# Where the weights of 72 TensorE products lie in SBUF, relative to the moving operands

## The chip, the cores and the metric

The kernel runs on one core of a Trainium2 chip. The metric is the device time of one execution in microseconds, the median of several runs. Profiles come from one execution recorded by the hardware profiler; its times are counted from the start of its span.

## What is computed

One decoder layer on 1024 prompt rows and 64 sample rows (1088 tokens in all, model width 1024). Cut to what matters here:

```python
a, q, k, v, g_a, g_b = split(rms_norm(x, ln1) @ w_in)
A = pooled(a) @ w_pa                       # causal multi-scale pooling
B = attended(q, k, v) @ w_pb               # dilated sliding-window attention, three groups
h = x + (sigmoid(g_a) * A + sigmoid(g_b) * B) @ w_o
y = h + square(relu(rms_norm(h, ln2) @ w_up)) @ w_down
```

The parts of interest are the gates `g_a`, `g_b` (1024 by 2048 weights) and the up projection `w_up` (1024 by 4096). All is float32 outside; the products are made of pairs of reduced-precision parts.

## The kernel before

**Precision.** Each float32 operand is split into a high part in a rounded format and a low part with the rest (`split`, L116 on ScalarE and L117 on VectorE). A product then takes three passes: high by high, high by low, low by high (`PASSES`).

**Seven products for eight.** The gate and the up projection are computed by a block scheme of the Strassen-Winograd kind. Tokens are cut into two halves (544 each) and the 1024 input channels into two halves (four tiles of 128 channels each); a panel of 256 output columns is cut into two tiles of 128. Each panel takes products of a weight block (128 columns by four channel tiles) with a token block. The products are named by their moving operand:

- `11` and `21`: blocks of the normed input, first token half. They lie in the two tiles `act` (high and low), whose channel tiles are 1088 words apart.
- `22`: a block of the second token half; `T1`: a sum of token blocks written in place of another one. Both lie in `act` too, 544 words further on.
- `T2`, `T3` and `T4`: further sums of token blocks. They lie outside `act`, four channel tiles of 544 words each, one after the other: T2 and T3 in `places`, T4 in a tile of its own (`gt4` in the gate stage, `t4`, shown as `t`, in the up stage).

One product (`products`, through `by_halves`, L1292) is 24 matmuls: two runs of twelve, the first for 264 tokens, the second for the other 280; in each run three passes over four channel tiles. Every matmul is preceded by its own load of weights (128 by 128), which the profile shows as PEld.

**Stages.** Attention and the first products of the gates share the time to 445 us. From there eight gate panels run with the products T1, T2, T3, 22 and T4 each. Then come the two branch projections (`pab`), the output projection (`ph`, L200) and the up projection: first the products 11 and 21 of panels 0 to 7, then T1, T2, T3, 22 and T4 of those eight, then panels 8 to 15 with all seven products in the order 11, T1, 21, T2, T3, 22, T4. The down projection (`pd`, L2069) ends the kernel.

**Where the weights lie.** `put_weights` writes a block's high and low parts into a spot of 1152 words; there are five spots, two in tiles of their own (`gapart` for the gates, `apart` for the up projection) and three in `places`. Inside a spot the four channel tiles of the high part start at `at + step * k`, those of the low part 128 words after them. The table `W_AT` gives `at` and `step` by product. The source of a block is a quarter of a weight panel or a sum of two quarters that VectorE has made.

**What sets the order.** TensorE's order is written out by hand: a queue of products, whose weights are prepared three products ahead (`run(ahead=3)`) and whose raw panels are asked for about seven products ahead. PSUM tiles are drained behind each product by ScalarE or VectorE.

Addresses below are counted in float32 words along a partition. The tiles `act`, `places`, `gapart`, `apart`, `gt4` and `t4` of the moving operands and weights all start at multiples of 64 words, as do the spots.

Of the kernel before, what the change touches and what calls it, by code (L numbers as in the profile page):

```python
# [15 lines left out]
P = 128  # L16
# [21 lines left out]
def decoder_step(ctx, tc, i, o):  # L38
# [76 lines left out]
    def split(dst_hi, dst_lo, src):  # L115
        ins = s_.activation(dst_hi, src, AF.Copy)  # L116
        v_.tensor_tensor(dst_lo, src, dst_hi.bitcast(F32), op=ALU.subtract)  # L117
        return ins
# [14 lines left out]
    def gate_quarter(f, a):  # L133
        return gate_panel(f).rearrange("p (k n) -> p k n", k=KD)[:, 4 * a:4 * a + 4, :P]
# [8 lines left out]
    def line_up(src, name, *after, width=None):  # L143


        wt = places[:, place[0] % 3]
        place[0] += 1
        width = width or src.shape[1]
        for a, key in zip(range(0, width, 512), after):
            coming_up.append(dict(width=width, src=src, name=name, a=a, key=key, wt=wt, raw=None))  # L150
        ask_ahead()
        return wt
# [33 lines left out]
    def behind_pe(ins, mm=None):  # L186

        tc.add_manual_dep(ins.ins, (mm or last_mm[0]).ins.name,
                          mybir.DependencyInfo(mybir.DependencyClass.Sync, mybir.DependencyReason.DATA), reason="pace")
# [349 lines left out]
    ap = pb.enter_context(tc.tile_pool(name="att", bufs=1, reuse_waits="tile"))  # L539
# [596 lines left out]
    for g in (2, 1, 0):  # L1136
# [42 lines left out]
        for blks in ((8, 0), (1,), (2,), (3,), (4,), (5,)) + (((6, 7),) if g else ((6,), (7,))):  # L1179
# [7 lines left out]
            elif not g and 3 in blks:  # L1187
                wg_first = line_up(lambda a: gate_quarter(a // 512 % 2, a // 1024), "ga0",
                                   *((0, 7, j) for j in (0, 0, 1, 1)), width=2048)
# [98 lines left out]
    def by_halves(out, terms, lhs, rhs, first=True, between=None):  # L1288

        for c in range(2):  # L1290
            for n, term in enumerate(terms):
                last_mm[0] = t_.matmul(out[c], lhs(*term), rhs(*term, c), start=(first and n == 0),  # L1292
                                       stop=(n == len(terms) - 1), skip_group_check=not first)
            if between:
                between()

    TERMS = [(a, b, k) for a, b in PASSES for k in range(4)]

    def products(x, A, Bv, first, between=None):
        by_halves(x, TERMS, lambda a, b, k: A[a][:, k], lambda a, b, k, c: Bv(b, k, c), first, between)  # L1300

    def put(t, src, marks):
        marks.append(split(t[:, 0], t[:, 1], src))
        return t

    W_AT = {"11": (8, 256), "21": (8, 256), "T1": (40, 256), "22": (40, 256), "T2": (8, 288), "T3": (8, 288), "T4": (8, 288)}

    def weights_at(at):
        return spots[:, at:at + 1152]

    def put_weights(t, src, marks, key):
        at, step = W_AT[key]
        if len(src.shape) == 2:
            src = by_tile(src)
        hi, lo = (bass.AP(tensor=t.tensor, offset=t.offset + at + P * s, ap=[t.ap[0], [step, 4], [1, P]]) for s in range(2))
        marks.append(split(hi, lo, src))
        return hi, lo

    queue, lazy, loads = [], [], {}
# [33 lines left out]
    def row_tile(n, name):  # L1353
        return rr(rows_p, [P, H], F32, name=f"g{n}_{name}", tag=f"g{n}", bufs=2)
# [65 lines left out]
    def put_gate(src, key):  # L1420
        spot[0] += 1
        return put_weights((apart + [weights_at(1152 * n) for n in (2, 1, 0)])[(spot[0] - 1) % 5], src, marks_g, key)
# [7 lines left out]
    by_tile = lambda t: t.rearrange("p (k n) -> p k n", n=P)  # L1430

    def gate_group(f):
# [34 lines left out]
        def post4():  # L1467
# [3 lines left out]
        loads.setdefault(max(0, len(queue) - 4), []).append(get_back)  # L1471
        enqueue(lambda: summed(1, quarter(f, 1, 0), quarter(f, 1, 1), ALU.add),
                lambda A: products(fresh(5), A, B["T1"], True), post5, (lambda: load_gate(f)) if f else None, 7)
        enqueue(lambda: summed(2, by_tile(sums[1]), quarter(f, 0, 0), ALU.subtract),
                lambda A: products(fresh(6), A, B["T2"], True), post6)
        enqueue(lambda: summed(3, quarter(f, 0, 0), quarter(f, 1, 0), ALU.subtract),
                lambda A: products(fresh(7), A, B["T3"], True), post7)
        enqueue(lambda: summed(4, quarter(f, 0, 1), by_tile(sums[2]), ALU.subtract),
                lambda A: products(outs(q["x5"]), A, B["22"], False), post3)
# [10 lines left out]

    def put_first(n):
        if n < 4:
            return [by_tile(wg_first[:, s, 512 * n:512 * n + 512]) for s in range(2)]
        if n < 16:
            w = put_weights(weights_at(1152 * ((n + 1) % 3)), raw_first.pop(n), marks_g, "11")
            behind_pe(marks_g[-1])
            return w
# [4 lines left out]
    for n in range(3):  # L1502
        ready[n] = put_first(n)
    for n, (f, a) in enumerate(order):
        fetch_first(n + 5)
        if a == 0:
            open_x[f] = bank_pair(f"pg{f}")
        products(open_x[f], ready.pop(n), B["21" if a else "11"], a == 0, between=step)
        ready[n + 3] = put_first(n + 3)
        t = row_tile(1 + a, f)  # L1510
        for c in range(2):
            s_.copy(t[:, part(c)], open_x[f][c])
        dma_st(g_d[f, 0][:, half(0)] if a else pg_d[f], t)
        if n in (3, 5, 7, 9):
            split_sums((n - 3) // 2)
        if n in (0, 1, 4, 6):
            fetch_sums((0, 1, 4, 6).index(n))
        if n % 4 == 3 and psx is None and not active and not waiting:
            finish_attention()
        if psx is not None and n > 8:  # L1520
            prepare_main()
        if n == 13:
            for f in range(8):
                gate_group(f)
            for n_prep in range(3):
                got[n_prep] = queue[n_prep][0]()
        if n == 14:
            for load in loads.pop(0):
                load()
# [106 lines left out]
    at = len(queue)  # L1636
# [116 lines left out]
    def put_up(src, key):  # L1753
        spot[0] += 1
        t = put_weights(up_spots[spot[0] % 5], src, marks_f, key)
        in_time(marks_f[-1])
        return t
# [340 lines left out]
    for g, n_rows in ((2, 30), (1, 21), (0, 30)):  # L2098
        src, dst = i[f"cache_kv{g + 1}"], o[f"kv{g + 1}_sample"]
# [111 lines left out]
```

## Time and profile before

| What | us |
|---|---|
| Median of three runs | 1410.89 |
| Lowest and highest run | 1408.71, 1411.37 |
| The profiled execution | 1410.39 |
| Its span | 1408.6 |
| First product of the gates | 384.8 |
| Gate panels with T1, T2, T3, 22, T4 | 444.92 to 565.30 |
| Branch projections | 565.30 to 637.0 |
| Output projection | 637.0 to 734.8 |
| Up projection, products 11 and 21 of panels 0 to 7 | 734.8 to 784.44 |
| The other five products of these panels | 784.44 to 904.82 |
| Panels 8 to 15, all seven products | 904.82 to 1072.52 |
| Down projection | 1072.52 to about 1404 |

How the views are read: PE is TensorE's matmuls and PEld its loads of weights. A matmul's row gives its duration of some 280 to 290 ns, but matmuls follow each other every 120 to 130 ns and overlap, so what counts is the time from the start of one to the start of the next, or from the start of one product to that of the next. In the timeline, rows of equal instructions are merged under the form of the first, so a row of 24 holds 12 matmuls of 264 columns and 12 of 280. Names stand without their numbers: `pg` and `pz` are PSUM tiles of the gates and of the up projection, and the names behind the arrow are the tiles that hold the moving operand and the weights.

### The profile page before, as it was taken

Reading aid. Unit: us, or ns where it says so; the run is one execution under the profiler, and the core shown is the slowest. Engines: PE = TensorE matmul, PEld = TensorE weight load, DVE = VectorE, ACT = ScalarE, POOL = GpSimd, SP = SyncE. Lnnn points to the kernel's source line nnn. Section 1 sums busy time; section 2 is a strip of 40 time slices with the busy share of each in tenths; the row PEclk is TensorE's granted clock in tenths of the full one; section 3 lists DMA queues with packets and bytes.
Section 4 is the critical chain, followed back from the end, with each engine's and each line's share of the span. In section 5 each row is a group of like instructions: output and inputs, shape, how many; then the busy total and the mean of one; then the engine's idle time right before and its main releaser. Section 6 shows DMA issues by size and latency. Waiting matters only on the chain.

```text
span 1408.6 us, 29517 instructions
## 1 busy us (share of the span) xinstructions
PE 1397.0 (99%) x11101; PEld 1348.7 (96%) x11101; DVE 970.1 (69%) x1766; ACT 758.8 (54%) x1962; POOL 233.9 (17%) x330
## 2 busy tenths in 40 slices
PE   9999999999999999999999999999999999999998
PEld 9988887888999999999999999999999999999998
DVE  7788675676776767876468678665665686664565
ACT  8557755777865233564336455554554544443443
POOL 0722265466500100000001000000000000000100
PEclk9999999999999999999999999999999999999999
DMA  6322778745377777975458668856658987777674
GB/s 214 117 96 103 219 212 220 195 140 145 105 253 228 252 227 238 315 240 171 140 199 278 230 224 267 266 191 220 237 196 286 326 276 260 228 247 228 200 265 168
DMA packets 184541, 303.58 MB, mean 216 GB/s; under 512 B 26567, under 2 KB 90509, under 8 KB 182350
## 3 DMA queue, kind: packets, MB, share of 16 engines
q1 hardware_dynamic: 181326, 258.04, 57.3%
q0 software_dynamic: 3072, 43.65, 9.4%
q8 instruction: 87, 1.43, 0.4%
q14 instruction: 56, 0.46, 0.1%
HBM read 231.55 MB, written 113.73 MB: 245 GB/s over the span
## 4 chain that ended last, share of the span: by engine, by line
PE 92%; DMA 3%; DVE 2%; ACT 1%; POOL 1%; SPq 1%; issue 1%; DVEq 0%; POOLq 0%; ACTq 0%
PE pz L1292 24%; PE pd L2069 24%; PE pg L1292 12%; PE ph L200 7%; PE pab L1292 5%; PE pqk L200 5%; PE pv L200 3%; PE a L328 3%; PE pq L200 1%; PE pk L200 1%; DMA raw_qkv<-in_w_in_dram 1%; DMA pcv<-in_cache_kv_dram 1%; PE pog0b L717 1%; PE sg0b L684 1%; PE tpg0b L703 0%
## 5 line engine op out<-in xcount | busy, mean ns | idle before, releaser
L2069 PE MATMUL pd<-places 128*128 128x272 f32 x2688 | 331.7, 287 | 0.0
L2069 PEld LDWEIGHTS pd<-places 128*128 128x128 f32 x2688 | 331.6, 188 | 0.0
L116 ACT ACTIVATE places<-raw_d 128x544 fp32r<-128x544 f32 (+1 forms) x176 | 111.3, 647 | 159.5 <-DMA raw_d<-z_d 58.6
L117 DVE TENSOR_TENSOR places<-raw_d,places 128x544 fp32r<-128x544 f32 (+1 forms) x176 | 123.1, 713 | 93.3 <-ACT places L116 91.3
L2109 POOL DMA_DIRECT2D out_kv_sample_dram<-in_cache_kv_dram x96 | 47.1, 490 | 794.6 <-ACT places L116 582.2
L1292 PE MATMUL pz<-act,places 128*128 128x280 f32 (+1 forms) x1080 | 139.4, 287 | 0.0
L1292 PEld LDWEIGHTS pz<-act,places 128*128 128x128 f32 x1080 | 135.9, 188 | 0.0
L200 PE MATMUL ph<-act,places 128*128 128x280 f32 (+1 forms) x768 | 96.6, 287 | 0.0
L200 PEld LDWEIGHTS ph<-act,places 128*128 128x128 f32 x768 | 96.0, 188 | 0.1
L1292 PE MATMUL pg<-act,places 128*128 128x264 f32 (+1 forms) x576 | 75.6, 288 | 0.0
L1292 PEld LDWEIGHTS pg<-act,places 128*128 128x128 f32 x576 | 72.6, 188 | 0.6 <-issue 0.3
L1292 PE MATMUL pz<-places,apart 128*128 128x264 f32 (+1 forms) x528 | 68.7, 289 | 0.0
L1292 PEld LDWEIGHTS pz<-places,apart 128*128 128x128 f32 x528 | 67.3, 188 | 0.0
L200 PE MATMUL pqk<-places,act 128*128 128x512 f32 x240 | 60.6, 402 | 0.0
L1292 PE MATMUL pz<-act,apart 128*128 128x264 f32 (+1 forms) x456 | 59.0, 287 | 0.0
L1292 PEld LDWEIGHTS pz<-act,apart 128*128 128x128 f32 x456 | 57.5, 188 | 0.1
L200 PE MATMUL pv<-places,act 128*128 128x256 f32 x384 | 51.7, 292 | 2.3 <-DVE places L117 2.3
L200 PEld LDWEIGHTS pqk<-places,act 128*128 128x128 f32 x240 | 44.8, 192 | 9.6
L646 POOL TENSOR_TENSOR mr<-ms,mhalf 128x4 f32<-128x4 f32 (+2 forms) x39 | 53.2, 1365 | 3.1
L851 POOL TENSOR_TENSOR pck<-pck,qs 128x256 f32<-128x256 f32 x64 | 47.0, 766 | 32.1 <-DMA pck<-in_cache_kv_dram 20.7
L200 PEld LDWEIGHTS pv<-places,act 128*128 128x128 f32 x384 | 48.5, 198 | 3.4 <-DVE places L117 2.5
L328 PE MATMUL a<-act,places 128*128 128x384 f32 (+1 forms) x288 | 50.5, 333 | 0.7 <-ACT act L306 0.7
(431 smaller groups left out, 2841.1 us busy)
## 6 DMA issues: line engine op xcount, KB each, us to landing
out_kv_sample_dram<-in_cache_kv_dram POOLq DMA_DIRECT2D x72, 480.0 KB, 4.9
raw_d<-z_d SPq DMA_DIRECT2D x112, 272.0 KB
z_d<-t SPq DMA_DIRECT2D x80, 272.0 KB
raw_d<-in_w_down_dram SPq DMA_DIRECT2D x80, 256.0 KB
raw_u<-in_w_up_dram SPq DMA_DIRECT2D x64, 256.0 KB
raw_qkv<-in_w_in_dram SPq DMA_DIRECT2D x36, 256.0 KB
pck<-in_cache_kv_dram SPq DMA_DIRECT2D x32, 256.0 KB
pcv<-in_cache_kv_dram SPq DMA_DIRECT2D x32, 256.0 KB
```

Source lines behind the costliest of these rows:

```text
L116: ins = s_.activation(dst_hi, src, AF.Copy)
L117: v_.tensor_tensor(dst_lo, src, dst_hi.bitcast(F32), op=ALU.subtract)
L200: last_mm[0] = t_.matmul(out, lhs(a, k), rhs(b, k), start=(j == 0), stop=(j == len(terms) - 1))
L328: last_mm[0] = t_.matmul(pts[m][:, :n], wt[:, a, kk, m * P:(m + 1) * P], act4[b][kk][:, :, part4(c)], start=(p == 0 and kk == 0), stop=(p ...
L646: last_norm[0] = g_.tensor_tensor(r[:n, :H], ms[:n, :H], mhalf[:n, :H], op=ALU.pow)
L684: t_.matmul(sc[e][:, hp, j * P:(j + 1) * P], qT[rows, hp, :], kT[rows, 2 + hp, :], start=True, stop=True)
L717: t_.matmul(po[e * HD:(e + 1) * HD, hp, :], vr[:, h * HD:(h + 1) * HD], pTs[e][:, hp * nk + j, :], start=(j == 0), stop=(j == nk - 1))
L851: ins = g_.tensor_tensor(out, *others, op=ALU.mult)
L1292: last_mm[0] = t_.matmul(out[c], lhs(*term), rhs(*term, c), start=(first and n == 0), stop=(n == len(terms) - 1), skip_group_check=not first)
L2069: last_mm[0] = t_.matmul(outs(chain[t], Q)[c], A[:, a, t * P:(t + 1) * P], Z[:, b, c], start=(fresh and f == 0 and n == 0), stop=(f == NG ...
L2109: ins = g_.dma_start(d, a)
```

## The change

The weights of T2, T3 and T4 get other places inside their spots. Before, their four channel tiles start at 8, 296, 584 and 872 (8 and steps of 288). Now they start at 40, 584, 296 and 840: tile k of the four is written as a pair (k // 2, k % 2), with steps of 256 and 544. The low parts stay 128 words behind. The weights of 11, 21, T1 and 22 stay where they were; they are only addressed by pairs too.

```diff
     def products(x, A, Bv, first, between=None):
-        by_halves(x, TERMS, lambda a, b, k: A[a][:, k], lambda a, b, k, c: Bv(b, k, c), first, between)
+        by_halves(x, TERMS, lambda a, b, k: A[a][:, k // 2, k % 2], lambda a, b, k, c: Bv(b, k, c), first, between)
...
-    W_AT = {"11": (8, 256), "21": (8, 256), "T1": (40, 256), "22": (40, 256), "T2": (8, 288), "T3": (8, 288), "T4": (8, 288)}
+    W_AT = {"11": (8, 256), "21": (8, 256), "T1": (40, 256), "22": (40, 256), "T2": (40, 544), "T3": (40, 544), "T4": (40, 544)}
...
-        hi, lo = (bass.AP(tensor=t.tensor, offset=t.offset + at + P * s, ap=[t.ap[0], [step, 4], [1, P]]) for s in range(2))
-        marks.append(split(hi, lo, src))
+        pairs = [[2 * step, 2], [step, 2]] if step == 256 else [[256, 2], [step, 2]]
+        hi, lo = (bass.AP(tensor=t.tensor, offset=t.offset + at + P * s, ap=[t.ap[0], *pairs, [1, P]]) for s in range(2))
+        marks.append(split(hi, lo, src.rearrange("p (a b) n -> p a b n", b=2)))
...
-            return [by_tile(wg_first[:, s, 512 * n:512 * n + 512]) for s in range(2)]
+            return [wg_first[:, s, 512 * n:512 * n + 512].rearrange("p (a b n) -> p a b n", a=2, b=2) for s in range(2)]
```

On every engine the order of the instructions is the same as before. Of the splits, those of T2, T3 and T4 (72 on ScalarE and 72 on VectorE) now write a pattern of 2 by 2 by 128 words per partition where they wrote one of 4 by 128; the others, with evenly spaced tiles, keep their form. No tile moves, and no wait or transfer is added or taken away.

## The prediction

> **What bounds the kernel now.** I read the page's head first, then its line of granted clock and its chain that ended last.
>
> ```profile
> span 1408.6 us, 29517 instructions
> PE 1397.0 (99%) x11101; PEld 1348.7 (96%) x11101; DVE 970.1 (69%) x1766; ACT 758.8 (54%) x1962; POOL 233.9 (17%) x330
> PEclk9999999999999999999999999999999999999999
> PE 92%; DMA 3%; DVE 2%; ACT 1%; POOL 1%; SPq 1%; issue 1%; DVEq 0%; POOLq 0%; ACTq 0%
> ```
>
> TensorE is busy for 99% of the span at full clock, and 92% of the chain is its own. A busy matmul row says nothing of how densely matmuls follow each other, so the next view is the table of stages (busy time of each engine in stretches that I cut at the starts of products).
>
> ```profile
> 421.13:444.92 23.79, 23.79 (x194) 23.79 (x193) 19.45 (x31) 17.05 (x37) 0.00 (x0) 1.00 0.77 256
> 748.76:784.44 35.68, 35.68 (x290) 35.68 (x289) 33.12 (x38) 26.88 (x39) 1.46 (x3) 1.00 0.91 301
> 444.92:565.30 120.38, 120.38 (x963) 120.38 (x961) 80.90 (x123) 37.50 (x60) 8.50 (x17) 1.00 0.72 234
> 784.44:904.82 120.38, 120.38 (x962) 120.38 (x961) 88.70 (x138) 59.08 (x95) 3.89 (x8) 1.00 0.70 233
> 904.82:1072.52 167.70, 167.70 (x1346) 167.70 (x1345) 106.00 (x161) 85.19 (x136) 12.16 (x25) 1.00 0.65 221
> 1072.52:1404.00 331.48, 331.48 (x2690) 331.47 (x2688) 212.68 (x316) 152.99 (x253) 17.02 (x35) 1.00 0.77 249
> ```
>
> The columns are the stretch, its length, then busy time (and instructions) of PE, PEld, DVE, ACT and POOL, clock and DMA. Rows one and two hold products 11 and 21 alone: 8 and 12 products of 24 matmuls (the counts include matmuls across the edges), so 23.79 / 8 = 2.974 us and 35.68 / 12 = 2.973 us each. Rows three to five are the stages in which the products T2, T3 and T4 stand: 8 gate panels of five products, 8 up panels of five, 8 of seven. There 120.38 / 40 = 3.010 and 167.70 / 56 = 2.995 us per product, though PE never stops there, DVE is busy 74% at most and ACT 51%. What limits these stages is the spacing of matmuls. The timeline (start, length, instruction, count) shows which ones are wide; first gate panels, then one late up panel:
>
> ```profile
> 456.94 3.19 PE L1292 MATMUL pg<-gt,places 128*128 128x264 f32 x24
> 459.97 3.14 PE L1292 MATMUL pg<-act,gapart 128*128 128x264 f32 x24
> 462.94 3.20 PE L1292 MATMUL pg<-places,gapart 128*128 128x264 f32 x24
> 465.98 3.19 PE L1292 MATMUL pg<-places 128*128 128x264 f32 x24
> 469.01 3.14 PE L1292 MATMUL pg<-act,places 128*128 128x264 f32 x24
> 471.99 3.19 PE L1292 MATMUL pg<-gt,places 128*128 128x264 f32 x24
> 475.02 3.14 PE L1292 MATMUL pg<-act,gapart 128*128 128x264 f32 x24
> ...
> 904.82 3.14 PE L1292 MATMUL pz<-act,places 128*128 128x264 f32 x24
> 907.80 6.13 PE L1292 MATMUL pz<-act,apart 128*128 128x264 f32 x48
> 913.76 6.19 PE L1292 MATMUL pz<-places 128*128 128x264 f32 x48
> 919.79 3.14 PE L1292 MATMUL pz<-act,places 128*128 128x264 f32 x24
> 922.76 3.20 PE L1292 MATMUL pz<-t,apart 128*128 128x264 f32 x24
> ```
>
> From start to start, T4 (moving gt) takes 3.03 us, T1 (moving act) 2.97, T2 3.04, T3 3.03, product 22 (act again) 2.98, T4 3.03. In the late panel T2 and T3 together take 6.03 us and the four products on act 2.97 to 2.98 each. All have the same shapes. **The three products with sums as moving operands are slower by about 0.055 us each, 2.3 ns per matmul, and there are 72 of them.**
>
> **The change, part by part.** It moves the weights of those 72 products by some words and nothing else: the order of instructions is the same on all engines, and no wait or transfer is added.
>
> What the new places do, in fp32 words along the partition and as remainders by 64 (all tiles concerned start at multiples of 64): the moving operand of tile k starts at 544k, so at 0, 32, 0, 32. The weights stood at 8, 296, 584, 872, so at 8, 40, 8, 40: always 8 from their own moving operand, and 40 from that of the matmul before. Now they stand at 40, 584, 296, 840, so at 40, 8, 40, 8: 40 from their own and 8 from the one before. In the second token half the moving start is 264 words further, which makes it 32 and 0. For 11, 21, T1 and 22 the panels on act step by 1088, a multiple of 64, and both distances are 8 (first half) or 0 (second).
>
> Which of the two distances meets in time? The load of the weights runs beside the matmul before:
>
> ```profile
> 901.53 0.42 PE L1292 MATMUL pz<-act,places 128*128 128x280 f32 x2
> 901.66 0.81 PEld L1292 LDWEIGHTS pz<-t,places 128*128 128x128 f32 x6
> 901.79 0.77 PE L1292 MATMUL pz<-t,places 128*128 128x264 f32 x5
> ```
>
> The first load for T4 begins at 901.66, one spacing ahead of T4's first matmul (901.79), so as the last matmul of the product before begins. So the distance to the preceding moving operand is the one in play. Does 32 cost anything with no change of tile or step? The output projection answers. It has constant steps; by the code its first half has 264 columns at distance 0 and 280 at 56, its second 280 at 32 and 264 at 8. Groups kept apart by shape, first half (window 637 to 684.96), then second (704.8 to 734.8):
>
> ```profile
> L200 PE MATMUL ph<-act,places 128*128 128x280 f32 x192 | 25.9, 290 | 0.0
> L200 PE MATMUL ph<-act,places 128*128 128x264 f32 x192 | 24.6, 284 | 0.0
> ...
> L200 PE MATMUL ph<-act,places 128*128 128x280 f32 x120 | 16.5, 293 | 0.0
> L200 PE MATMUL ph<-act,places 128*128 128x264 f32 x120 | 15.2, 282 | 0.0
> ```
>
> Busy time by count: 280 columns take 134.9 ns at 56 and 137.5 at 32, so 2.6 more; 264 columns take 128.1 at 0 and 126.7 at 8, so 1.4 less. (Each run's last matmul overhangs by the same amount, so differences count.) The surcharge of T2 to T4 has the size of that of distance 32.
>
> *The sum.* If every product takes 2.974 us, the gate stage takes 40 x 2.974 = 118.96 us, 1.42 less; the first up panels the same, 1.42 less; the late ones 56 x 2.974 = 166.54, 1.16 less. Together 4.0 us. T1 and 22 read 2.975 rather than 2.974 on average, and there are 64 products on act in these stages: 0.1 us stays. **I take 3.9 us.** Bounds: by the projection's rows, where distance 0 was 1.4 ns dearer than 8, the 280 columns (32 to 0) may gain only 2.6 - 1.4 = 1.2 ns and the 264 columns (40 to 8) 2.6, which makes 864 x 3.8 ns = 3.3 us. At best they come down to the densest matmuls here, the down stage's 331.48 / 2688 = 123.3 ns or 2.960 us per 24: 408.46 - 64 x 2.975 - 72 x 2.960 = 4.9 us.
>
> *Edges between products.* T1's last matmul met T2's first weights at 32 and meets them at 0 now; where 21 stands ahead of T2 (8 late panels) it is the reverse. That is one matmul each of 2 to 3 ns, some 20 ns: nothing.
>
> *The 72 splits.* Each writes a pattern of 2x2x128 where it wrote 4x128, on ACT and on DVE. The trace has no such form, so I bound it from the rows of the old one:
>
> ```profile
> L116 ACT ACTIVATE gapart<-sm_g x16: 626/633/637, 440.3 to 548.8; 128x512 fp32r<-128x512 f32 x16
> L117 DVE TENSOR_TENSOR gapart<-sm_g,gapart x16: 681/692/694, 441.6 to 549.5; 128x512 fp32r<-128x512 f32 x16
> ```
>
> Below: 633 and 692 ns unchanged. Above: twice as long, 72 x 0.69 = 50 us more on DVE, spread over 408 us in which it is busy 276: it still keeps up, and PE would not see it. The cover is the lead: the first such split ends near 442.3 and its product begins at 444.92. Only a split longer by over 2.6 us would stop PE. I take zero.
>
> *What is late next.* PE comes 1% earlier to its inputs in these stages. It has no idle time there that the stage table shows, and DMA engines are busy 65 to 72%, so I expect nothing to become late; the down stage then starts 3.9 us earlier and keeps its length.
>
> The profiled execution took 1410.39 us, 1.79 more than its span; less 3.9 that is 1406.5. The runs' median is 1410.89, 0.5 above it, which gives 1407.0. I say **1406.8 us**.
>
> **The rivals.**
>
> *The moving operand itself is at fault (no change).* The slow products differ from the fast ones also in that their moving starts alternate between 0 and 32 and lie in other tiles. If the surcharge hangs on that, nothing moves: 1410.4 to 1410.9. For it: no fast product in this trace has such an operand. Against it: gt and places, two different tiles, give the same 3.03, and the projection's 280 columns pay as much on act with a constant step. The Trainium skill speaks for this rival: SBUF — State Buffer, section "Who interferes with whom", says that TensorE reads moving operand and weights through two independent ports and never waits on anyone; by that rule distance cannot matter and the sum would be 0. The projection's 2.6 ns is hard to square with the rule, but is one pair of rows. 18%.
>
> *Own distance is what costs (slower).* In the projection both distances are the same number, so its 2.6 ns could belong to the matmul's own weights, and the slow T products could owe theirs to the alternating starts. Then the change puts own distance 40 or 32 on 1728 matmuls that now have 8 or 0: up to 1728 x 2.6 ns = 4.5 us slower, 1414.9. It decides as soon as over half of the surcharge belongs to the own distance. Against it: the load stands beside the matmul before, as quoted. 6%.
>
> *Partial gain.* The lower bound, 3.3 us, or less if only one column width gains; it lies inside the forecast's case.
>
> **How the numbers follow.** Forecast 76%, no change 18%, slower 6%. The forecast's own range is 1410.39 - 4.9 = 1405.5 to 1410.89 - 3.3 = 1407.6, and with the runs' scatter (1408.71 to 1411.37) 1404.9 to 1409. To hold 8 in 10 I extend it into the second case, to 1410.5. A difference of 0.2%, 2.8 us, is about what a measurement of this kernel can tell from no change; the forecast clears it by 1 us only, so of its 76% I give 66 to faster and 10 to within. Faster 0.66; within 0.28; slower 0.06.
>
> **What would show it.** Right: in the timeline T2, T3 and T4 take 2.97 to 2.98 from start to start, a gate panel 14.87 instead of 15.05, and the down stage begins near 1068.6 instead of 1072.5 while attention, projection and down stages keep their lengths. The second half of the output projection keeps its 137.5. Wrong: T products at 3.03 (the operand is at fault) or about 3.09 (own distance costs); or 2.97 with idle PE before some of them, which would mean weights or panels now come late.

## The result and the profile after

| | before | changed |
|---|---|---|
| Median of 20 runs each, us | 1409.24 | 1405.74 |
| Lowest and highest, us | 1405.62, 1411.62 | 1403.44, 1410.25 |
| Profiled execution: time, span, us | 1410.39, 1408.6 | 1405.47, 1403.7 |

The ratio of the times is 0.9977 with a 95% interval of 0.9969 to 0.9986: 3.2 us faster, between 2.0 and 4.4 (the two medians differ by 3.50). Runs of one kernel differ by more than that, so the parts have to be read inside the traces. Two lines of the changed kernel's page, the busy times of the engines and the granted clock (9 is 90% or more): TensorE is still busy for 99% of the span.

```profile
PE 1392.2 (99%) x11101; PEld 1343.0 (96%) x11101; DVE 965.2 (69%) x1766; ACT 758.0 (54%) x1962; POOL 234.2 (17%) x330
PEclk9999999999999999999999999999999999999999
```

The stage table of the changed kernel, cut at the same instructions as before: the gate panels, the second round of the up panels 0 to 7, the panels 8 to 15. The granted clock, third from the end, is 1.00 in all three, as it was before.

```profile
442.53:561.78 119.25, 119.25 (x962) 119.25 (x961) 80.81 (x122) 36.95 (x59) 8.52 (x17) 1.00 0.73 235
781.20:900.45 119.25, 119.25 (x962) 119.25 (x961) 88.22 (x137) 58.86 (x95) 3.90 (x8) 1.00 0.72 235
900.45:1067.43 166.98, 166.98 (x1346) 166.98 (x1345) 106.24 (x161) 85.00 (x136) 12.17 (x25) 1.00 0.66 222
```

The three stages took 120.38, 120.38 and 167.70 us and now take 119.25, 119.25 and 166.98: 1.13 + 1.13 + 0.72 = **2.98 us**. The spans differ by 4.9. Of the rest, 2.39 us lie ahead of the gate panels (they begin at 442.53 instead of 444.92), where the change touches nothing; in the six traces whose kernels are the same up to there, this stage starts between 440.5 and 445.1, so that is scatter. About 0.5 us is given back: 0.28 between the gates and the up panels, 0.19 behind the late panels.

The timeline of a gate panel in the changed kernel, T1 to T4 and the next T1 (start, length, instruction, count):

```profile
457.43 3.14 PE L1292 MATMUL pg<-act,gapart 128*128 128x264 f32 x24
460.41 3.15 PE L1292 MATMUL pg<-places,gapart 128*128 128x264 f32 x24
463.40 3.16 PE L1292 MATMUL pg<-places 128*128 128x264 f32 x24
466.39 3.14 PE L1292 MATMUL pg<-act,places 128*128 128x264 f32 x24
469.37 3.14 PE L1292 MATMUL pg<-gt,places 128*128 128x264 f32 x24
472.34 3.13 PE L1292 MATMUL pg<-act,gapart 128*128 128x264 f32 x24
```

From start to start T2 takes 2.99 us (3.04 before), T3 2.99 (3.03), T4 2.97 (3.03); T1 and 22 stay at 2.97 to 2.98. Nearly all of the gain sits in the three products that the change touches; on the average of the eight panels, 22 alone adds 0.006 us (2.979 to 2.973). T4 reaches the products on `act`; T2 and T3 stop some 0.02 us short of them.

### The profile page after: what moved, and what is told of

Read it like the earlier page. It is cut to its first block, busy times and chain, and to the rows that moved or that the text cites. A ratio compares the mean times of both kernels' runs of the same rounds, so it can differ in the third digit from the quotient of the medians.

```text
span 1403.7 us, 29517 instructions
## 1 busy us (share of the span) xinstructions
PE 1392.2 (99%) x11101; PEld 1343.0 (96%) x11101; DVE 965.2 (69%) x1766; ACT 758.0 (54%) x1962; POOL 234.2 (17%) x330
## 4 chain that ended last, share of the span: by engine, by line
PE 92%; DMA 3%; DVE 1%; ACT 1%; POOL 1%; issue 1%; SPq 0%; DVEq 0%; POOLq 0%; ACTq 0%
PE pz L1292 24%; PE pd L2070 24%; PE pg L1292 12%; PE ph L200 7%; PE pqk L200 5%; PE pab L1292 5%; PE pv L200 4%; PE a L328 3%; DMA raw_qkv<-in_w_in_dram 2%; PE pq L200 1%; PE pk L200 1%; PE sg0b L684 1%; PE pog0b L717 1%; PE tpg0b L703 0%; POOL mr L646 0%
## 5 line engine op out<-in xcount | busy, mean ns | idle before, releaser
L1292 PE MATMUL pab<-ab,places 128*128 128x264 f32 (+1 forms) x384 | 50.5, 287 | 0.0
```

## The experiments

Seven kernels were run. All are variants of the changed kernel unless another is named, and all but the last have a single run, the profiled one, since what counts is the length of single products. (Their times, of one run each: the first three 1411.0, 1408.44 and 1410.28 us beside 1413.96 for the kernel before; the third kernel of the distances 1414.29.)

### Distance or pattern

```diff
-... "T2": (40, 544), "T3": (40, 544), "T4": (40, 544)}
+... "T2": (8, 544), "T3": (8, 544), "T4": (8, 544)}
```

> The weights of T2, T3 and T4 keep the new order of their channel tiles (0, 2, 1, 3) and the new 2x2x128 write, but start at 8, so the next matmul's weights are again 40 (264 columns) and 32 (280 columns) from the running moving operand, and 8 and 0 from their own. If the distance to the next matmul's weights decides, T2 to T4 take 3.03 us each again and the three stages last 120.4, 120.4 and 167.7 us, as before the change. If the order of the channel tiles or the form of the write made the gain, they stay at 2.98 to 2.99 us and 119.3, 119.3 and 167.0 us.

The stage table and the timeline of a gate panel of this kernel (T2, T3, 22, T4 in this order, then T1 of the next panel):

```profile
445.13:565.51 120.38, 120.38 (x962) 120.38 (x961) 81.42 (x123) 37.52 (x60) 8.50 (x17) 1.00 0.72 233
784.65:905.03 120.38, 120.38 (x962) 120.38 (x961) 89.45 (x139) 59.17 (x95) 3.89 (x8) 1.00 0.72 233
905.03:1073.04 168.01, 167.94 (x1346) 167.75 (x1345) 106.71 (x162) 85.97 (x138) 12.16 (x25) 1.00 0.66 221
...
463.16 3.20 PE L1292 MATMUL pg<-places,gapart 128*128 128x264 f32 x24
466.20 3.19 PE L1292 MATMUL pg<-places 128*128 128x264 f32 x24
469.22 3.14 PE L1292 MATMUL pg<-act,places 128*128 128x264 f32 x24
472.20 3.19 PE L1292 MATMUL pg<-gt,places 128*128 128x264 f32 x24
475.23 3.14 PE L1292 MATMUL pg<-act,gapart 128*128 128x264 f32 x24
```

T2 is back at 3.04, T3 at 3.02, T4 at 3.03, and the first two stages at 120.38 us to the last digit (the third has 168.01 instead of 167.70: in it one load of weights waits 0.3 us for ScalarE). With the order of the channel tiles and the written pattern of the changed kernel, a shift of 32 words alone gives the old time. The distance carries the whole gain, the pattern nothing. The weights' own starts, as remainders by 64, are 8, 40, 8, 40 here and 40, 8, 40, 8 in the changed kernel, so what differs is how they lie to the moving operand. It also bears on which distance counts: here and in the kernel before, a matmul is 8 or 0 from its own weights and 40 or 32 from the next ones and is slow; in the changed kernel it is the other way round and it is fast. For these products the two always change together; T1, whose two distances are equal, bears on that below.

### Every product at its own distance

Three kernels give each product another start, so that one execution shows many distances.

```diff
-W_AT = {"11": (8, ...), "21": (8, ...), "T1": (40, ...), "22": (40, ...), "T2": (40, ...), "T3": (40, ...), "T4": (40, ...)}
+first:  11 8, 21 16, T1 24, 22 56, T2 56, T3 72, T4 48
+second: 11 24, 21 32, T1 72, 22 32, T2 24, T3 8, T4 56
+third:  11 12, 21 4, T1 44, 22 48, T2 44, T3 52, T4 36
```

> Each product gets a distance of its own (264 columns / 280 columns): 11 keeps 8/0, 21 gets 16/8, T1 56/48, 22 24/16, T2 24/16, T3 40/32, T4 16/8. If the distance decides whatever the moving operand is, T3 takes 3.03 us, and all others 2.97 to 2.99 us unless 24/16 or 56/48 is itself dear. If the surcharge belongs to T2 to T4 as such, their moving operands and steps, all three take the same time whatever the distance, and 11, 21, T1 and 22 stay at 2.974.

> The other points: 11 gets 24/16, 21 gets 32/24, T1 40/32, 22 0/56, T2 56/48, T3 40/32, T4 24/16. If the distance decides, T1, whose moving operand lies in act with a constant step and took 2.975 us in both kernels, now takes 3.03 us, and so does T3, while T2 and T4 stay near 2.98; 21 at 32/24 is between, near 3.00. If the moving operand decides, T1 stays at 2.975.

> Finer points (264 columns / 280 columns): 11 12/4, 21 4/60, T1 12/4, 22 16/8, T2 12/4, T3 20/12, T4 4/60. In the first sweep 16/8 gave 2.958 us for T4 but 3.024 for 21, 24/16 2.994 to 3.003, 56/48 3.008 to 3.023. If a distance counts by itself, T1, T2 and 11 at 12/4 agree within 0.01 us. If it counts together with the step of the moving operand, T2 at 12/4 and T3 at 20/12 come below 2.97, and 11, T1 and 22 above 2.99.

One gate panel of the first kernel (T1, T2, T3, 22, T4, then the next T1):

```profile
456.84 3.18 PE L1292 MATMUL pg<-act,gapart 128*128 128x264 f32 x24
459.86 3.16 PE L1292 MATMUL pg<-places,gapart 128*128 128x264 f32 x24
462.86 3.19 PE L1292 MATMUL pg<-places 128*128 128x264 f32 x24
465.89 3.17 PE L1292 MATMUL pg<-act,places 128*128 128x264 f32 x24
468.89 3.12 PE L1292 MATMUL pg<-gt,places 128*128 128x264 f32 x24
471.85 2.40 PE L1292 MATMUL pg<-act,gapart 128*128 128x264 f32 x18
```

The same of the second:

```profile
457.31 3.16 PE L1292 MATMUL pg<-act,gapart 128*128 128x264 f32 x24
460.31 3.17 PE L1292 MATMUL pg<-places,gapart 128*128 128x264 f32 x24
463.32 3.19 PE L1292 MATMUL pg<-places 128*128 128x264 f32 x24
466.35 3.14 PE L1292 MATMUL pg<-act,places 128*128 128x264 f32 x24
469.33 3.16 PE L1292 MATMUL pg<-gt,places 128*128 128x264 f32 x24
472.33 2.90 PE L1292 MATMUL pg<-act,gapart 128*128 128x264 f32 x22
```

And of the third:

```profile
461.02 3.14 PE L1292 MATMUL pg<-act,gapart 128*128 128x264 f32 x24
464.00 3.17 PE L1292 MATMUL pg<-places,gapart 128*128 128x264 f32 x24
467.01 3.18 PE L1292 MATMUL pg<-places 128*128 128x264 f32 x24
470.02 3.18 PE L1292 MATMUL pg<-act,places 128*128 128x264 f32 x24
473.04 3.20 PE L1292 MATMUL pg<-gt,places 128*128 128x264 f32 x24
476.08 2.12 PE L1292 MATMUL pg<-act,gapart 128*128 128x264 f32 x16
```

From start to start in the gate panels, in us, by the distance of the next weights (264 columns / 280 columns):

| Distance | on act (T1, 22) | sums (T2, T3, T4) |
|---|---|---|
| 4/60 | | T4 3.04 |
| 8/0 (the changed kernel) | 2.97 to 2.98 | 2.97 to 2.99 |
| 12/4 | T1 2.98 | T2 3.01 |
| 16/8 | 22 3.02 | T4 2.96 |
| 20/12 | | T3 3.01 |
| 24/16 | 22 3.00 | T2 3.00, T4 3.00 |
| 40/32 | T1 3.00 | T3 3.03, twice |
| 56/48 | T1 3.02 | T2 3.01 |
| 0/56 | 22 2.98 | |

Products on `act`, fast in all kernels so far, slow down at most other places of their weights, so the surcharge belongs to no moving operand. T1, with both distances at 40/32, takes 3.00 instead of 2.97, so 40/32 from the own weights is not what makes the changed kernel fast. T3 at 40/32 keeps its 3.03, with its weights at 72 in the first kernel and at 8 in the second, 64 words apart. Three expectations failed. "Elsewhere near 2.98" is wrong: most places cost 0.02 to 0.06 us, and for the sums 8/0 is a narrow good one. T1 at 40/32 was to take 3.03 and took 3.00 in the gates, behind T4, but 3.06 in the late panels of the same trace, behind 11. And a distance isn't a price by itself: 16/8 is the best place for a sum and a bad one for 22. Whether that lies in the step of the moving operand, in the distance to the own weights or in the products ahead, these kernels don't separate. The third kernel doesn't follow either of its two theories.

### The product ahead

Before the change, T2 took 3.04 us in the gates but 3.00 in the late up panels, at the same distances. There it stands behind 21 (its first load 0 words from the running operand), elsewhere behind T1 (32 words). Two kernels, one from each side of the change, put T2 behind T1 in the late panels too:

```diff
-        for n, p in enumerate(groups[f]):
+        for n in (0, 2, 1, 3, 4, 5, 6) if f >= FIRST else range(7):
+            p = groups[f][n]
```

> The kernel before, with the late panels' products in the order 11, 21, T1, T2, T3, 22, T4, as in the other panels. Before, T2 at the same distances of 40 and 32 took 3.04 us behind T1 (first load 32 from the running operand) and 3.00 us behind 21 (first load 0 away). If the spacing that a run settles on depends on how it is entered, T2 in the late panels goes from 3.00 to 3.04 us, now that it stands behind T1. If it depends on the tiles in which T2's weights and operand lie in the late panels, it stays at 3.00.

> The same order in the changed kernel. There T2 took 2.99 us behind T1 and 3.005 behind 21, and T1 and 21 took 2.983 in the late panels (each entering the other at 32). If the entry counts: T2 2.992, 21 2.974, and the late stage about 8 x 0.03 = 0.2 us shorter than the 166.98 us of the changed kernel. If not, no product changes.

The timeline of panel 9, first of the kernel before (T2, T3, then 22), then the same three rows with the new order, behind one row with 21 and T1:

```profile
934.73 3.16 PE L1292 MATMUL pz<-places 128*128 128x264 f32 x24
937.73 3.19 PE L1292 MATMUL pz<-places,apart 128*128 128x264 f32 x24
940.75 3.14 PE L1292 MATMUL pz<-act,apart 128*128 128x264 f32 x24
```

```profile
929.21 6.23 PE L1292 MATMUL pz<-act,places 128*128 128x264 f32 x48 [0.70 <-ACT t L1856]
935.28 3.19 PE L1292 MATMUL pz<-places 128*128 128x264 f32 x24
938.31 3.20 PE L1292 MATMUL pz<-places,apart 128*128 128x264 f32 x24
941.35 3.14 PE L1292 MATMUL pz<-act,apart 128*128 128x264 f32 x24
```

T2 goes from 3.00 to 3.03 and T3 from 3.02 to 3.04, with every address of theirs unchanged; only what stands ahead of them differs. Taken matmul by matmul from the same traces, it is the first twelve of T2 that change, from 120.0 to 122.7 ns each; the second twelve keep 129.8 to 130.0. The pair of the changed kernel, in its own order and in the new one:

```profile
930.27 3.17 PE L1292 MATMUL pz<-places 128*128 128x264 f32 x24
933.27 3.14 PE L1292 MATMUL pz<-places,apart 128*128 128x264 f32 x24
936.25 3.14 PE L1292 MATMUL pz<-act,apart 128*128 128x264 f32 x24
```

```profile
930.01 3.15 PE L1292 MATMUL pz<-places 128*128 128x264 f32 x24
933.00 3.16 PE L1292 MATMUL pz<-places,apart 128*128 128x264 f32 x24
936.00 3.14 PE L1292 MATMUL pz<-act,apart 128*128 128x264 f32 x24
```

T2 goes from 3.00 to 2.99, as in the gates; T3 from 2.98 to 3.00, as in the gates (2.99) too. So the 0.02 us by which T3 misses the other products doesn't hang on the tiles it uses: it has it or loses it in the same place, by what ran ahead. T2 misses them in both orders. The expected 0.2 us less for the late stage did not come: what T2 gains T3 loses, and in the new order 21 waits for ScalarE's drain of the product before (0.70 us of idle in the row above, eight times). So 21 takes 3.08 instead of the expected 2.974, the late stage lasts 174.67 us instead of 166.98 (175.84 instead of 167.70 in the kernel before), and the kernels took 1417.26 and 1410.82 us.

### The best place found, for all three sums

```diff
-... "T2": (40, 544), "T3": (40, 544), "T4": (40, 544)}
+... "T2": (48, 544), "T3": (48, 544), "T4": (48, 544)}
```

> The changed kernel with the weights of T2, T3 and T4 at 48 instead of 40, so 16 and 8 from the running operand. If all three behave as T4 did in the first sweep, they take 2.958 us: 16 panels x 0.089 and 8 late panels x up to 0.08 less, 1.4 to 2.0 us less than the changed kernel, a ratio of about 0.9965 to the kernel before. If T4's 2.958 came from how it was entered there, the time is that of the changed kernel, ratio 0.9977.

Stages, and T2, T3, 22, T4 and T1 of a gate panel:

```profile
443.70:562.90 119.20, 119.20 (x962) 119.20 (x961) 80.93 (x122) 37.44 (x60) 8.50 (x17) 1.00 0.73 234
782.75:901.96 119.21, 119.21 (x962) 119.21 (x961) 89.37 (x139) 59.02 (x95) 3.89 (x8) 1.00 0.73 237
901.96:1068.68 166.72, 166.72 (x1346) 166.72 (x1345) 106.15 (x161) 84.67 (x135) 12.16 (x25) 1.00 0.67 221
...
461.58 3.15 PE L1292 MATMUL pg<-places,gapart 128*128 128x264 f32 x24
464.57 3.14 PE L1292 MATMUL pg<-places 128*128 128x264 f32 x24
467.55 3.14 PE L1292 MATMUL pg<-act,places 128*128 128x264 f32 x24
470.52 3.15 PE L1292 MATMUL pg<-gt,places 128*128 128x264 f32 x24
473.51 2.75 PE L1292 MATMUL pg<-act,gapart 128*128 128x264 f32 x21
```

T2 2.99, T3 2.98, T4 2.99: T4's 2.96 did not come along. In the first of the three kernels it stood behind a 22 that had been moved; here it stands behind the usual one. Again the difference is in the first twelve matmuls, 117.0 ns there and 119.5 here, with 129.5 in the second twelve of both. The three stages take 405.13 us against 405.48 in the changed kernel, 0.35 less (0.26 of it in the late panels, where T2 takes 2.97 instead of 3.00), and the ratio to the kernel before is 0.9979 (0.9963 to 0.9995) against 0.9977 (0.9969 to 0.9986): no difference that these runs tell.

## Why the prediction held, and where it was off

- **The bound.** Right: PE never stopped in these stages before or after, and the time came out of the spacing of matmuls.
- **Which distance counts.** Right: next weights at 8 or 0 instead of 40 or 32 is what gains. The pattern kernel shows it with nothing else changed, and the rival with the own distance, forecast at up to 4.5 us slower, is out. The rival with the moving operand is out by it too, though the distance isn't the whole price either. What the prediction drew from the Trainium skill (SBUF — State Buffer, "Who interferes with whom"), that TensorE's two read ports make the distance irrelevant, does not fit this kernel: a shift of the weights by 32 words, with nothing else altered, moves three stages by 408.77 - 405.48 = 3.3 us, 0.3 of which is the wait for ScalarE.
- **The sum.** The term that was mis-sized is "if every product takes 2.974 us". It gave 1.42 + 1.42 + 1.16 = 4.0, of which 3.9 was taken; measured is 1.13 + 1.13 + 0.72 = 2.98. T2 and T3 settled at 2.99, so 16 panels lack 2 x 0.02 each, 0.6 us. In the late panels T2 stood at 3.00 already and stayed there, where 0.03 less was counted eight times: another 0.2. The remaining 0.2 us is spread over 21, T1 and T4 of the late panels, which take some 0.01 more than the 2.974 counted. The step behind it that failed is "Edges between products ... nothing": the prediction let the product ahead touch one matmul, and in the experiment on the order it changed the spacing of the first twelve. By the starts of single matmuls, the second twelve (280 columns, 32 to 0) gained about what was counted, from 129.8 ns to 127.7 to 128.1 in T2, T3 and T4 of the gates and in the late T2. The first twelve (264 columns, 40 to 8) gained 1.6, 0.8 and 2.5 ns in T2, T3 and T4 of the gates, and in the late T2, behind 21, they lost 2.3 (120.0 to 122.3). The forecast's own lower bound of 3.3 us was too high for the same reason: both bounds took the spacing as a function of the distance alone. The late T2 at 3.00 lay open in the trace, in the quoted row with T2 and T3 in 6.03 us, and was not taken as a sign of it.
- **The price read from the output projection.** This reading was wrong. The second window holds a product that begins behind the matmuls of `bc`, at 704.74 us, and its second matmul starts 340 ns after its first. Without that product, from 710.8 to 734.8 us, the row of the kernel before is

```profile
L200 PE MATMUL ph<-act,places 128*128 128x280 f32 x96 | 13.0, 291 | 0.0
```

This makes 13.0 / 96 = 135.4 ns beside 134.9, so about 0.5 ns for distance 32 and not 2.6. That the 2.6 had the size of the surcharge of T2 to T4 was chance, and the lower bound and the price of the own distance were worked out from it. What the 280 columns of T2 to T4 really paid, some 2 ns, stands only in their own matmuls.
- **The rest.** The splits cost nothing that shows, as said: their medians into `gapart` stay at 633 and 692 ns. (The lead of 2.6 us that covered them was read at T1, which is not one of the three; T2 begins 3 us later.) A gate panel takes 119.25 / 8 = 14.91 us, where 14.87 was forecast. "Nothing becomes late" holds but for one load of weights in the branch projections, which now waits 0.2 us for VectorE. The down stage was to begin 3.9 us earlier; counted from the start of the gate panels it begins 2.7 earlier (624.90 instead of 627.60).
- **The time.** 1406.8 was forecast and 1405.74 measured. A good part of the closeness is luck: the gain in the three stages was 1 us less than counted, but the kernel before has a median of 1409.24 over 20 runs, 1.65 below the 1410.89 of the three runs that the forecast started from.

## What to carry to other kernels

Where a stream of matmuls with a new weight load each is the bound, compare the start-to-start times of products of the same shape: differences of 1 or 2% that no wait explains can come from where the weights lie relative to the operand that streams while they are loaded. Try places one product at a time in one execution, but trust a place only behind the neighbour it will have, since the product ahead changes what it gives. And where the gain is smaller than the scatter between runs, compare stages between the same two instructions.

## What the runs showed of the hardware that was not expected

The spacing of matmuls repeats to the hundredth of a microsecond: 120.38 us for two different stages in two kernels. It is not set by the distance alone; the same 24 matmuls at the same addresses took 3.00 or 3.03 us by what ran ahead of them, and it was the first twelve that changed (120.0 or 122.7 ns). Sums with their next weights at 16/8 took 2.96 us behind one neighbour and 2.99 behind another, while 4 words off the good place 8/0 they took 3.01 to 3.04. What in the chip makes these differences wasn't tried and stays open. Most of the scatter that the traces locate lies ahead of the gate panels: in six kernels that are the same up to there, these began between 440.5 and 445.1 us.
